# The output projection of a hybrid encoder layer: three PSUM banks in turn instead of two

## The chip, the cores and the metric

One core of a Trainium2 chip runs the whole layer as one program. The metric is the device time of one execution in microseconds (us), given as the median of several runs. A profile is one further execution, with a record of every instruction.

## What is computed

The layer normalises its input, projects it once into queries, keys, values and gates, runs windowed attention and a state-space scan beside each other, merges the two branches, and ends with an output projection, a residual sum and a second normalisation. Shapes: 2048 tokens, 1024 channels, float32.

```python
h = rms_norm(x, norm_gain[l])
proj = jnp.einsum('bsd,de->bse', h, w_in[l])
...
attn = windowed_gqa(q, k, v, attn_sink[l], rel_bias_table) * jax.nn.silu(z_attn)
y = s5_bidirectional(u_ssm, ...)
y = jax.nn.gelu(y)
y = y * jax.nn.sigmoid(jnp.einsum('bsc,ce->bse', y, w_glu[l]) + b_glu[l])
ssm = y * jax.nn.silu(z_ssm)
merged = jax.nn.sigmoid(g_attn) * jnp.einsum('bsc,cd->bsd', attn, w_branch_attn[l]) \
       + jax.nn.sigmoid(g_ssm) * jnp.einsum('bsc,cd->bsd', ssm, w_branch_ssm[l])
x = x + jnp.einsum('bsd,de->bse', merged, w_out[l])
return rms_norm(x, final_norm_gain)
```

## The kernel before

Every float32 matmul is made of three: each operand is split into a high and a low part of a narrower type, and high x high, high x low and low x high are summed in PSUM. The tokens are cut into four blocks of 512. The program goes through the input projections with normalisation, scan and attention worked in beside them, and then, for the blocks in the order 2, 3, 1, 0, through three stages:

- `glu(b)` (L1503): a 512 x 512 projection of the scan's output and the elementwise work around it, most of it on VectorE.
- `branch(b)` (L1530): both branch projections, gated and summed into `mh` and `ml` (the high and low part of `merged`).
- `outp(b)` (L1580): the output projection, which the change touches. For four tiles of 128 tokens (`t`) and two halves of the channels (`n`) it runs a group of 24 matmuls (L1592 to L1594, eight steps of three) into one PSUM bank. VectorE then adds the bank to the residual tile `xr` (L1599), and `finish` (L1627) squares, normalises and stores the tile on ScalarE, GpSimd and VectorE in later turns.

The loop at the end of the program runs `branch(b)`, then `glu` of the next block, then `outp(b)`, so that the weights and the gates of the next block are under way. Beside `branch` runs `gelu_prep` of the next block (L1415), and beside `outp(b)` runs `attn_prep` of the next block (L1466): it loads four tiles `ar` (L1474), copies each on ScalarE into a high part `ah` (L1484) and subtracts on VectorE for the low part `al` (L1485). The last `outp` (block 0) has no such companion.

The order of each engine's queue is the order of the program text; side work is dealt into it by `tick` and `turn`, which the matmul loops call at fixed points. An engine works off its queue in that order, so an addition L1599 stands behind whatever VectorE work was issued before it.

PSUM has eight banks, each of 128 x 512 float32. They are handed out by name, as the two lines below say: three called `pj`, two each called `s1` and `s2`, and one called `s3`. A new tile of a name takes the name's next bank, and its first matmul waits until the bank's last reader is done. In the profile all of `s1`, `s2` and `s3` appear as `s`. `s3` is used by attention's values alone (`values`, L1154; last read in `result`, L1179).

```python
PSB = {"pj": 3, "s1": 2, "s2": 2, "s3": 1}
...
return ps.tile([128, 512], F32, tag=tag, name=tag, bufs=PSB[tag])
```

Of the kernel before, what the change touches and what calls it, by code (L numbers as in the profile page):

```python
# [37 lines left out]
def kernel(  # L38
# [43 lines left out]
    def bank(tag):  # L82
        return ps.tile([128, 512], F32, tag=tag, name=tag, bufs=PSB[tag])
# [22 lines left out]
    def tick():  # L106

        flush()
        due = [f for n, f in laters if n <= 1]
        laters[:] = [(n - 1, f) for n, f in laters if n > 1]  # L110
        for f in due:
            f()
        turn()

    def turn():

        for sd in sides:
            if sd["done"]:
                continue
            sd["credit"] += 0.5 * sd["rate"]  # L120
            while sd["credit"] > 0.0:
                try:
                    sd["credit"] -= 0.5 if next(sd["gen"]) is HALF else 1.0
                except StopIteration:
                    sd["done"] = True
                    break
# [1119 lines left out]
    with tc.manual_schedule():  # L1246
# [55 lines left out]
        s2 = ExitStack()  # L1302
# [272 lines left out]
        def load_xr(b, t, q=None):  # L1575
            r0 = b * BLK + t * 128
            xrs[b, t] = ftile([128, D], F32, "xr", "xr", 3)
            (q or nc.sync).dma_start(out=xrs[b, t], in_=x[r0:r0 + 128, :])

        def outp(b, last):  # L1580
            mh, ml = mx.pop(b)
            for t in range(4):
                r0 = b * BLK + t * 128
                xr = xrs.pop((b, t))
                if t + 1 < 4:
                    load_xr(b, t + 1)
                for n in range(2):
                    pt = bank("s2")
                    cs = slice(n * 512, (n + 1) * 512)
                    for k in range(KD):  # L1590
                        ts_ = slice(t * 128, (t + 1) * 128)
                        PE.matmul(pt, mh[k][:, ts_], wo[0, n][:, k], start=k == 0, stop=False)  # L1592
                        PE.matmul(pt, mh[k][:, ts_], wo[1, n][:, k], start=False, stop=False)  # L1593
                        PE.matmul(pt, ml[k][:, ts_], wo[0, n][:, k], start=False, stop=k == KD - 1)  # L1594
                        if k == 3:
                            tick()
                        elif k % 4 == 1:
                            turn()
                    V.tensor_tensor(xr[:, cs], xr[:, cs], pt, ALU.add)  # L1599
                    if last and t == 3:  # L1600
                        finish_half(xr, r0, n)
                    tick()
                if not (last and t == 3):
                    finish(xr, r0)
# [3 lines left out]
        def finish_half(xr, r0, n):  # L1608

            cs = slice(n * BLK, (n + 1) * BLK)  # L1610
            if n == 0:
                sl_["sm"] = ftile([128, 3], F32, "sml", "sml")
                sl_["xf"] = ftile([128, D], F32, "xr", "xf", 3)
            sm, xf = sl_["sm"], sl_["xf"]
            A.activation(ttile("jk").bitcast(BF16)[:, 0:BLK], xr[:, cs], AF.Square, accum_out=sm[:, n:n + 1])
            V.tensor_tensor(xf[:, cs], xr[:, cs], fin["fg"][:, cs], ALU.mult)
            if n == 0:
                return
            V.tensor_tensor(sm[:, 2:3], sm[:, 0:1], sm[:, 1:2], ALU.add)
            V.tensor_scalar(sm[:, 2:3], sm[:, 2:3], 1.0 / D, 1e-6, ALU.mult, ALU.add)  # L1620
            Q.tensor_tensor(sm[:, 2:3], sm[:, 2:3], mhalf[:, 0:1], ALU.pow)
            V.tensor_scalar_mul(xf[:, 0:BLK], xf[:, 0:BLK], sm[:, 2:3])
            nc.sync.dma_start(out=out[r0:r0 + 128, 0:BLK], in_=xf[:, 0:BLK])
            A.activation(xf[:, BLK:D], xf[:, BLK:D], AF.Copy, scale=sm[:, 2:3])
            A.dma_start(out=out[r0:r0 + 128, BLK:D], in_=xf[:, BLK:D])

        def finish(xr, r0):  # L1627
            sm = ftile([128, 2], F32, "sm", "sm", 3)

            def f1():  # L1630
                jk = ttile("jk").bitcast(BF16)
                A.activation(jk, xr, AF.Square, accum_out=sm[:, 0:1])

            def f2():
                V.tensor_scalar(sm[:, 1:2], sm[:, 0:1], 1.0 / D, 1e-6, ALU.mult, ALU.add)  # L1635
                Q.tensor_tensor(sm[:, 1:2], sm[:, 1:2], mhalf[:, 0:1], ALU.pow)  # L1636

            def f3():
                V.scalar_tensor_tensor(xr, xr, sm[:, 1:2], fin["fg"], ALU.mult, ALU.mult)

            def f4():
                A.dma_start(out=out[r0:r0 + 128, :], in_=xr)

            f1()
            later(1, f2)
            later(2, f3)
            later(3, f4)
# [36 lines left out]
        for i, b in enumerate(BO):  # L1684
            nxt = BO[i + 1] if i + 1 < NBLK else None
            if nxt is not None:
                sg = add_side(gelu_prep(nxt, 1), 1.0)
            branch(b, nxt)
            if nxt is not None:
                drain(sg)  # L1690
            load_xr(b, 0, A)
            if nxt is not None:
                glu(nxt)
                sa = add_side(attn_prep(nxt, 1), 1.0)
            outp(b, nxt is None)
            if nxt is not None:
                drain(sa)
# [48 lines left out]
```

## Time and profile before

| | us |
|---|---|
| median of 3 runs | 1507.56 |
| lowest and highest run | 1506.02, 1509.10 |
| profiled execution | 1508.19 |
| span of the profiled execution, first to last instruction | 1506.4 |
| TensorE busy | 1418.1 |
| VectorE busy | 1041.8 |
| ScalarE busy | 659.9 |
| GpSimd busy | 637.9 |

The span of a profiled execution is a little shorter than its time, by what lies before the first and behind the last instruction. Busy times overlap, since the engines work beside each other. A group of instructions in the profile has its busy time, the mean of one in ns, and the idle time of its engine just before it, with the instruction that ended that idle time. Matmuls overlap: one takes 0.40 us by its record and the next starts 0.23 us behind it.

### The profile page before, as it was taken

The numbers are of one execution on the slowest core, as the hardware profiler recorded it, in microseconds if no ns is written. First come the engines' busy times: TensorE is split into PE (matmuls) and PEld (weight loads), VectorE is DVE, ScalarE is ACT, GpSimd is POOL, SyncE is SP. The second block draws the span as 40 slices with busy tenths as digits, with TensorE's granted clock in tenths as the row PEclk, the third lists the DMA queues.
The fourth block names the chain that finished last, engine by engine and source line by source line (L and its number), as shares of the span: only waits on it lengthen the run. The fifth ranks groups of instructions, "written<-read, shape, count | busy, mean of one in ns | idle before, by whom it ended". The sixth has DMA issues, their size and how long they took to land.

```text
span 1506.4 us, 19697 instructions
## 1 busy us (share of the span) xinstructions
PE 1418.1 (94%) x6933; PEld 1154.6 (77%) x6933; DVE 1041.8 (69%) x1954; ACT 659.9 (44%) x1213; POOL 637.9 (42%) x683
## 2 busy tenths in 40 slices
PE   7999779899999999899999999999988999999998
PEld 6787567777778777788888888888766877877886
DVE  2327977779788788647999998874577386385442
ACT  6332133433534444535666666754453243242111
POOL 5520187758678777622111111112376153252320
PEclk9999989989999999999999999999999999999999
DMA  8534222322332332554333333235776375375441
GB/s 264 157 98 95 64 81 72 100 91 76 113 105 88 109 105 88 152 175 127 92 91 92 101 96 91 90 102 148 211 212 193 98 196 181 114 182 166 117 122 70
DMA packets 240723, 185.47 MB, mean 123 GB/s; under 512 B 57921, under 2 KB 202433, under 8 KB 240625
## 3 DMA queue, kind: packets, MB, share of 16 engines
q10 hardware_dynamic: 118192, 107.89, 24.3%
q1 hardware_dynamic: 122432, 76.34, 17.1%
q8 instruction: 54, 0.88, 0.2%
q14 instruction: 45, 0.36, 0.1%
HBM read 126.56 MB, written 57.62 MB: 122 GB/s over the span
## 4 chain that ended last, share of the span: by engine, by line
PE 39%; DVE 26%; issue 7%; DMA 6%; ACT 5%; POOL 4%; ACTq 1%; DVEq 0%; POOLq 0%; SPq 0%
PE pj L220 7%; PE pj L222 7%; PE pj L221 7%; PE s L1592 3%; PE s L1593 3%; PE s L1594 3%; DVE Hl L891 2%; DMA yt<-yS 2%; DVE X L879 2%; PE s L1163 2%; DVE X L868 2%; PE s L1110 2%; DVE rt L867 2%; DVE X L870 2%; PE s L1147 2%
## 5 line engine op out<-in xcount | busy, mean ns | idle before, releaser
L155 POOL TENSOR_TENSOR wl<-raw,wh 128x256 fp32r<-128x256 f32 x380 | 355.0, 964 | 573.5 <-ACT wh L163 483.7
L220 PE MATMUL pj<-hh,wh 128*128 128x512 f32 x976 | 391.2, 401 | 0.0
L222 PE MATMUL pj<-hh,wl 128*128 128x512 f32 x976 | 385.7, 395 | 0.0
L221 PE MATMUL pj<-hl,wh 128*128 128x512 f32 x976 | 385.6, 395 | 0.0
L222 PEld LDWEIGHTS pj<-hh,wl 128*128 128x128 f32 x976 | 185.6, 190 | 41.0
L220 PEld LDWEIGHTS pj<-hh,wh 128*128 128x128 f32 x976 | 186.3, 191 | 34.0
L221 PEld LDWEIGHTS pj<-hl,wh 128*128 128x128 f32 x976 | 186.1, 191 | 34.3
L163 ACT ACTIVATE wh<-raw 128x1024 fp32r<-128x1024 f32 x96 | 100.7, 1051 | 23.4 <-DMA raw<-in_w_branch_ssm_dram 7.9
L1592 PE MATMUL s<-woh,mh 128*128 128x512 f32 x256 | 102.3, 400 | 6.7 <-DVE xr L1599 6.7
L1594 PE MATMUL s<-woh,ml 128*128 128x512 f32 x256 | 102.0, 398 | 0.0
L1593 PE MATMUL s<-wol,mh 128*128 128x512 f32 x256 | 101.9, 398 | 0.0
L1127 ACT ACTIVATE p<-p,sml 128x384 f32<-128x384 f32 (+1 forms) x128 | 75.8, 594 | 16.3 <-DVE sml L1123 16.1
L1636 POOL TENSOR_TENSOR sm<-sm,mhalf 128x1 f32<-128x1 f32 x15 | 8.3, 550 | 170.1 <-DVE sm L1635 133.4
L404 ACT ACTIVATE st<-pj,bg 128x512 f32<-128x512 f32 x64 | 43.8, 685 | 79.0 <-PE pj L222 69.3
L1111 DVE CUSTOM_DVE_ANT_0 p<-s,bias 128x384 f32<-128x384 f32 (+1 forms) x128 | 68.3, 535 | 13.7 <-PE s L1110 13.2
L1599 DVE TENSOR_TENSOR xr<-xr,s 128x512 f32<-128x512 f32 x32 | 21.9, 686 | 69.3 <-PE s L1594 69.3
L867 DVE TENSOR_TENSOR rt<-X,es 128x1020 f32<-128x1020 f32 x32 | 43.3, 1353 | 38.1 <-issue 14.4
L1152 DVE TENSOR_TENSOR pl<-s,ph 128x512 fp32r<-128x512 f32 x92 | 62.9, 683 | 4.2 <-ACT ph L1150 2.9
L1110 PE MATMUL s<-kst,qs 128*128 128x384 f32 (+1 forms) x256 | 65.7, 339 | 0.0
L1592 PEld LDWEIGHTS s<-woh,mh 128*128 128x128 f32 x256 | 48.5, 189 | 20.5 <-DVE xr L1599 8.9
L870 DVE TENSOR_TENSOR X<-X,rt 128x510 f32<-128x510 f32 x64 | 62.0, 1009 | 1.1
L891 DVE TENSOR_TENSOR Hl<-X,Hh 64x1024 fp32r<-64x1024 f32 x32 | 46.7, 1460 | 17.9 <-ACT Hh L886 17.4
(307 smaller groups left out, 3049.2 us busy)
## 6 DMA issues: line engine op xcount, KB each, us to landing
raw<-in_w_in_dram SPq DMA_DIRECT2D x59, 512.0 KB
gS<-st ACTq DMA_DIRECT2D x64, 256.0 KB
gt<-gS ACTq DMA_DIRECT2D x64, 256.0 KB
x<-in_x_dram SPq DMA_DIRECT2D x16, 512.0 KB
raw<-in_w_branch_attn_dram SPq DMA_DIRECT2D x32, 256.0 KB
raw<-in_w_branch_ssm_dram SPq DMA_DIRECT2D x32, 256.0 KB
out_dram<-xr ACTq DMA_DIRECT2D x15, 512.0 KB
xr<-in_x_dram SPq DMA_DIRECT2D x12, 512.0 KB
```

Of the source, the lines that this page charges most:

```text
L155: eng.tensor_tensor(lo[:, ks], r[:, ks], hi[:, ks].bitcast(F32), ALU.subtract)
L163: A.activation(res[0], r, AF.Copy)
L220: PE.matmul(pt, w[0][:, k], r[0][:, k], start=start and k == 0, stop=False)
L221: PE.matmul(pt, w[0][:, k], r[1][:, k], start=False, stop=False)
L222: PE.matmul(pt, w[1][:, k], r[0][:, k], start=False, stop=stop and k == kt - 1)
L870: V.tensor_tensor(X[:, :, r], X[:, :, r], t[:, :, r], ALU.add if r == back else ALU.subtract)
L891: V.tensor_tensor(H[1][rows], xv, H[0][rows].bitcast(F32), ALU.subtract)
L1110: PE.matmul(pt[:, 0:w], s["qs"][:, h], kst[:, r, kv, k0 * 128:k1 * 128], start=r == 0, stop=r == 1)
L1127: A.activation(p[:, h, 0:w], p[:, h, 0:w], AF.Exp, bias=nm[:, j:j + 1], accum_out=den[:, j:j + 1])
L1592: PE.matmul(pt, mh[k][:, ts_], wo[0, n][:, k], start=k == 0, stop=False)
L1593: PE.matmul(pt, mh[k][:, ts_], wo[1, n][:, k], start=False, stop=False)
L1594: PE.matmul(pt, ml[k][:, ts_], wo[0, n][:, k], start=False, stop=k == KD - 1)
```

## The change

The tile for a group of the output projection is no longer always a bank of the name `s2`. A group's number in its block is 2t + n; where that leaves 1 when divided by 3 the bank `s3` is taken.

```diff
@@ -1585,7 +1585,7 @@
                 if t + 1 < 4:
                     load_xr(b, t + 1)
                 for n in range(2):
-                    pt = bank("s2")
+                    pt = bank(("s2", "s3", "s2")[(2 * t + n) % 3])
                     cs = slice(n * 512, (n + 1) * 512)
                     for k in range(KD):
                         ts_ = slice(t * 128, (t + 1) * 128)
```

## Rows read from the trace of the kernel before

**Rows 1.** The page: TensorE's total, and the groups L1592 and L1599.

```profile
PE 1418.1 (94%) x6933; PEld 1154.6 (77%) x6933; DVE 1041.8 (69%) x1954; ACT 659.9 (44%) x1213; POOL 637.9 (42%) x683
...
L1592 PE MATMUL s<-woh,mh 128*128 128x512 f32 x256 | 102.3, 400 | 6.7 <-DVE xr L1599 6.7
...
L1599 DVE TENSOR_TENSOR xr<-xr,s 128x512 f32<-128x512 f32 x32 | 21.9, 686 | 69.3 <-PE s L1594 69.3
```

**Rows 2.** Stretches from:to: length, TensorE busy (instructions), granted clock, DMA; four `outp`.

```profile
1147.68:1196.25 48.57, 46.60 (x193) 0.96 0.37 123
1255.27:1302.26 46.99, 45.34 (x193) 1.00 0.37 123
1361.54:1409.93 48.39, 45.33 (x193) 1.00 0.36 120
1454.73:1499.52 44.79, 44.79 (x193) 1.00 0.17 59
```

**Rows 3.** Timeline of TensorE: start, duration, line, matmul, [idle before, releaser]; in `outp`.

```profile
1158.64 0.40 PE L1594 MATMUL s<-woh,ml 128*128 128x512 f32 x1
1161.01 0.50 PE L1592 MATMUL s<-woh,mh 128*128 128x512 f32 x1 [1.97 <-DVE xr L1599]
1161.35 0.40 PE L1593 MATMUL s<-wol,mh 128*128 128x512 f32 x1
...
1163.29 0.63 PE L1593 MATMUL s<-wol,mh 128*128 128x512 f32 x1
1163.72 0.63 PE L1594 MATMUL s<-woh,ml 128*128 128x512 f32 x1
...
1267.29 0.50 PE L1592 MATMUL s<-woh,mh 128*128 128x512 f32 x1 [0.67 <-DVE xr L1599]
...
1274.15 0.50 PE L1592 MATMUL s<-woh,mh 128*128 128x512 f32 x1 [0.99 <-DVE xr L1599]
...
1373.55 0.50 PE L1592 MATMUL s<-woh,mh 128*128 128x512 f32 x1 [0.65 <-DVE xr L1599]
...
1379.03 0.40 PE L1594 MATMUL s<-woh,ml 128*128 128x512 f32 x1
1381.84 0.50 PE L1592 MATMUL s<-woh,mh 128*128 128x512 f32 x1 [2.41 <-DVE xr L1599]
```

**Rows 4.** Stretches as in rows 2: behind the first stall, and around the longest.

```profile
1162.05:1165.42 3.37, 3.37 (x9) 0.50 1.02 406
...
1379.20:1382.60 3.40, 0.99 (x4) 1.00 0.02 6
```

**Rows 5.** Timeline of VectorE in `outp` of blocks 2, 3 and 1.

```profile
1160.27 0.68 DVE L1599 TENSOR_TENSOR xr<-xr,s 128x512 f32<-128x512 f32 x1
1166.35 0.69 DVE L1485 TENSOR_TENSOR al<-ar,ah 128x512 fp32r<-128x512 f32 x1 [5.39 <-ACT ah L1484]
1166.96 0.68 DVE L1599 TENSOR_TENSOR xr<-xr,s 128x512 f32<-128x512 f32 x1
...
1196.45 0.69 DVE L1599 TENSOR_TENSOR xr<-xr,s 128x512 f32<-128x512 f32 x1 [3.71 <-PE s L1594]
...
1273.41 0.68 DVE L1599 TENSOR_TENSOR xr<-xr,s 128x512 f32<-128x512 f32 x1
...
1381.10 0.68 DVE L1599 TENSOR_TENSOR xr<-xr,s 128x512 f32<-128x512 f32 x1
```

**Rows 6.** Timeline of ScalarE: the first `ah` in `outp` of block 1.

```profile
1379.83 0.63 ACT L1484 ACTIVATE ah<-ar 128x512 fp32r<-128x512 f32 x1 [7.65 <-DMA ar<-aS]
```

**Rows 7.** Timeline of TensorE: a stall outside `outp`, at the start of `glu`.

```profile
1246.30 0.50 PE L221 MATMUL pj<-gl,wh 128*128 128x512 f32 x1 [1.56 <-DVE gl L1446]
```

**Rows 8.** Line L1179: durations least/median/most, first and last start.

```profile
L1179 DVE TENSOR_TENSOR ob<-s,up x64: 408/417/421, 719.7 to 1017.3; 64x256 f32<-64x256 f32 x64
```

**Rows 9.** Stretches between the `outp`: length, VectorE busy (instructions), granted clock, DMA.

```profile
1196.25:1255.27 59.02, 44.12 (x53) 1.00 0.73 188
1302.26:1361.54 59.28, 44.18 (x53) 1.00 0.73 186
```

## The prediction

> **What bounds the kernel now.** I read the page first. TensorE is busy for 94% of the span [rows 1], so time is to be had only where it stands still or where its clock is low. The matmuls of the output projection (L1592) have 6.7 us of idle time in front of them, all put down to the addition L1599 that empties their PSUM bank; that addition in turn waits 69.3 us for TensorE over its 32 executions [rows 1]. Both at once means: on average VectorE is far ahead, and only in some places late.
>
> To see where, I cut out the four executions of `outp`, from the first matmul of each to the first one behind it, and read TensorE's busy time in each [rows 2]. They issue the same 192 matmuls each, and last 48.57, 46.99, 48.39 and 44.79 us. The last one (block 0) is without a gap: 44.79 us busy out of 44.79, so 44.79 / 192 = 0.2333 us from one matmul to the next, and 24 x 0.2333 = 5.60 us for a group (one bank). It has no `attn_prep` beside it. So the reader has the same work with and without the wait in one trace: the excess of the other three is 3.78 + 2.20 + 3.60 = 9.58 us.
>
> The timeline of TensorE shows what the excess is made of [rows 3]. In block 2 the last matmul of a group starts at 1158.64 and the next group's first at 1161.01: 2.37 us instead of 0.23, with another 0.11 us at the matmul behind it, so 2.25 us. This is more than the 1.97 us that the idle column gives, because the modelled end of a matmul (0.40 us behind its start) lies behind the point where the next could have begun. From 1162.05 to 1165.42 matmuls then start every 0.43 us [rows 3] at a granted clock of 0.50 [rows 4], the 1.2 GHz level: 8 intervals of about 0.19 us too much, 1.53 us. Together 3.78, the whole excess. Blocks 3 and 1 have two stalls each and no low clock: 0.94 + 1.26 us, and 0.92 + 2.68 us, counted in the same way. So there are five stalls, at the third group (1161.01, 1267.29, 1373.55) and twice at the fourth (1274.15, 1381.84).
>
> The timeline of VectorE says why the additions are late [rows 5]. The one of group 0 comes at 1160.27, behind the elementwise work that `glu` left queued; with two banks, group 2 needs that bank. The one of group 1 stands in VectorE's queue behind `al` (L1485), which waits for ScalarE's `ah`, and that for the load `ar` [rows 6]: VectorE idles 5.39 us before 1166.35, and the addition comes at 1166.96. Group 3 needs it. By the end of each `outp` VectorE waits for TensorE again, 3.71 us before the last addition [rows 5].
>
> **The change part by part.** Nothing is added or removed: the same matmuls, additions, loads and tiles, in the same order on every queue. Only the bank names change, and with them what the first matmul of a group waits for. The names of groups 0 to 7 are s2, s3, s2, s2, s3, s2, s2, s3. The two s2 banks alternate, five uses in a block, so every group waits for the addition three groups back instead of two.
>
> *Group 2 (third).* Its bank was last used in the block before, or is s3 itself, so the wait for group 0 goes: 2.25, 0.94 and 0.92 us. *Group 3* now needs group 0's addition. That starts at 1160.27 in block 2 and takes 0.69 us, while group 3 would begin at 1147.68 + 3 x 5.60 = 1164.48. It has 3.5 us to spare there, and the stalls of blocks 3 and 1 at this place, 1.26 and 2.68 us, go too. *Group 4* is what is late next: it needs group 1's addition, the one behind `al`. It would begin 22.40 us after the block's first matmul, at 1170.08, 1277.67 and 1383.94. The additions start at 1166.96, 1273.41 and 1381.10 [rows 5] and end 0.69 us later: 2.4, 3.6 and 2.2 us to spare. They are not moved by a faster TensorE, since what holds them is the load `ar` [rows 6]; nor does it start the load earlier, since that is issued by ScalarE in `glu`'s own sequence.
>
> *The low clock in block 2.* It follows the stall, the only idle time of TensorE since the block began, so without the stall I count the 1.53 us as gone. But an idle stretch does not always bring it: behind the longest stall (1379.03 to 1381.84) the clock stays at 1.00 [rows 4]. So which stalls pay this is not settled from run to run. The remaining stalls outside `outp`, such as the 1.56 us at 1246.30 [rows 7], come at other moments after the change, and one or two of them could pay 1.53 us each: 0 to +3.1 us. I take 0, since none of them does in these two blocks now.
>
> *The bank s3 itself.* Its last reader in attention (L1179) starts at 1017.3 [rows 8], 130 us before it is wanted, so its first use waits for nothing. A price for writing or emptying this bank rather than another is not shown for `outp`. The nearest row bounds it: block 0 changes its bank seven times without a gap [rows 2]. I take 0.
>
> *What follows `outp`.* The gain counts only if `branch` and `glu` start and end as much earlier. They are largely VectorE's work, 44.12 us busy out of 59.02 [rows 9], so VectorE could hold its end fixed. But VectorE itself starts `branch` waiting for TensorE [rows 5], so it starts earlier as well. The trace has a comparison: the two stretches between `outp`s last 59.02 and 59.28 us [rows 9], although the `outp` before the second was 1.58 us shorter than the one before the first [rows 2]. So a shorter `outp` gave back at most 0.26 of 1.58, a sixth. Of the 3.78 + 2.20 us that pass through such a stretch this is 0 to 1.0 us; I take 0. Behind the third, block 0 has a `branch` without preparation beside it, and the tail is unchanged.
>
> **Sum.** 2.25 + 1.53 + 2.20 + 3.60 = 9.58 us. The profiled execution took 1508.19 us (1506.4 us of span and 1.8 us around it), so 1498.6 us; it lies 0.6 us above the median of the runs, 1507.56, on which scale it is 1498.0. I give 1498.3.
>
> **The rivals.**
> *Given back in part.* The loads behind `branch` and `glu` (or `ar`, arriving later than the 2.2 us to spare) set the pace, and TensorE waits there instead. For it: VectorE is busy for three quarters of those stretches, and the addition of group 1 hangs on a load that took until 1379.83 with ScalarE waiting 7.65 us [rows 6]. Against it: the two equal stretches. With the one-sixth loss on all of it and two low-clock stretches of 1.53 us: 1498.3 + 1.6 + 3.1 = 1503.0; half of the gain lost gives the same.
>
> *It does not do what it says.* If the pool gave groups 2 and 3, and 5 and 6, the same s2 bank, each second one would wait for the addition just before it: 0.40 us to the end of the last matmul and 0.74 us from the addition to the next start (1160.27 to 1161.01), less 0.23, so 0.9 us, eight times: 7.3 us back, 1505.6, which is no change. Against it: in block 0 seven changes between the two s2 banks are without a gap, so the pool does alternate. Full cover elsewhere (all of the gain waited for later) gives 1507.5, no change as well.
>
> *Slower.* TensorE changes its bank with every group, and if each change cost enough to bring the clock down, `outp` would run partly at 1.2 GHz: 1.53 us for each low stretch as in block 2. It decides from (9.6 + 3.0) / 1.53, some eight such stretches among the 32 groups; one for every second group would be 1498.3 + 16 x 1.53 = 1522.8. Against it: block 0, seven changes, no gap, busy throughout [rows 2]. In the Trainium skill, "TensorE: Matmul & The Clock Gate", section "A second HAM failure mode: psum-queue depth-cycling", tells of such a kernel: cycling through PSUM banks idles TensorE a little between groups, and its clock swings between the two levels. By that rule this change, which cycles through more banks, would be the slower case; the trace does not agree, since the gaps here are those of a bank not yet empty, and more banks take them away.
>
> **How the numbers follow.** Forecast as summed, 1496 to 1501: 0.75. Given back in part, 1501 to 1505: 0.12. No change (either way): 0.06. Slower: 0.04. Faster still than 1496, when other runs than the profiled one pay the low clock more often: 0.03. A measurement of this kernel can tell about 0.2%, 3 us, from no change, so faster means below 1504.5: 0.75 + 0.03 + 0.10 = 0.88; same 0.08; slower 0.04. Range: below, the lowest run shown, 1506.02, less 9.6, is 1496.4, so 1496.0; above, it takes in the unknown costs up to half of their sum (1.0 and 3.1) and about half of the second case: 1502.5.
>
> **What would show it.** In the profile after: no wait of L1592 for L1599, or under 0.5 us in all; four `outp` stretches of 44.8 us each; no granted clock below 1.00 in them; the stretches between them still 59 us; the additions of groups 0 and 1 as late against the start of their block as now. Wrong would be a new wait before group 4 or 5, longer stretches between, or more low-clock matmuls in `branch` and `glu`.

## The result, and the profile after

The changed kernel takes 1498.02 us (median of 12 runs, 1496.32 to 1504.59), the kernel before in the same comparison 1506.76 us (12 runs, 1502.15 to 1510.3). The ratio is 0.995, with a 95% interval of 0.9937 to 0.9963: 8.7 us less by the medians, 7.5 us by the ratio, 5.6 to 9.5 us by its interval. The forecast was 1498.3 us.

The profiled execution took 1497.58 us, with a span of 1495.8 us. Both programs have the same instructions in the same order on every engine. So the two traces can be laid side by side stretch by stretch. Here are the four output projections of the changed kernel, which answer to [rows 2] (columns: from:to, length, TensorE busy and instructions, granted clock, DMA share and GB/s):

```profile
1146.29:1191.09 44.80, 44.80 (x194) 1.00 0.40 133
1250.53:1295.33 44.80, 44.80 (x194) 1.00 0.40 129
1354.49:1399.30 44.81, 44.81 (x194) 1.00 0.39 130
1444.09:1488.89 44.80, 44.80 (x193) 1.00 0.16 59
```

All four are alike now, busy throughout, at a granted clock of 1.00. Before they took 48.57, 46.99, 48.39 and 44.79 us. The difference, 3.77 + 2.19 + 3.58 = 9.54 us (0.01 more in the fourth), is the whole excess that the prediction had read off.

The page's groups, to be held against [rows 1]: idle time ahead of L1592 has gone from 6.7 us to nothing, and VectorE's wait for TensorE ahead of the addition from 69.3 to 60.0 us, by nearly what the groups were held up before.

```profile
L1592 PE MATMUL s<-woh,mh 128*128 128x512 f32 x256 | 101.3, 396 | 0.0
...
L1599 DVE TENSOR_TENSOR xr<-xr,s 128x512 f32<-128x512 f32 x32 | 21.9, 684 | 60.0 <-PE s L1594 60.0
```

TensorE's timeline in block 2 at the changes from group 1 to 2, 2 to 3 and 3 to 4 (start, duration, matmul; to be held against [rows 3]):

```profile
1157.25 0.40 PE L1594 MATMUL s<-woh,ml 128*128 128x512 f32 x1
1157.49 0.40 PE L1592 MATMUL s<-woh,mh 128*128 128x512 f32 x1
...
1162.85 0.40 PE L1594 MATMUL s<-woh,ml 128*128 128x512 f32 x1
1163.09 0.40 PE L1592 MATMUL s<-woh,mh 128*128 128x512 f32 x1
...
1168.45 0.40 PE L1594 MATMUL s<-woh,ml 128*128 128x512 f32 x1
1168.69 0.40 PE L1592 MATMUL s<-woh,mh 128*128 128x512 f32 x1
```

Each change takes 0.24 us, as any other matmul to the next. The additions are not any earlier. This is VectorE's timeline in block 1 (with the idle time before and its releaser in brackets), to be held against [rows 5]:

```profile
1365.76 0.68 DVE L1599 TENSOR_TENSOR xr<-xr,s 128x512 f32<-128x512 f32 x1
1373.32 0.69 DVE L1485 TENSOR_TENSOR al<-ar,ah 128x512 fp32r<-128x512 f32 x1 [6.88 <-ACT ah L1484]
1373.93 0.68 DVE L1599 TENSOR_TENSOR xr<-xr,s 128x512 f32<-128x512 f32 x1
```

The block begins at 1354.49, so the additions of groups 0 and 1 start 11.27 and 19.44 us into it. In the kernel before, the second one started 1381.10 - 1361.54 = 19.56 us in. VectorE is as late as it was, and behind the same wait; only nobody waits for it.

The stretches between the output projections, to be held against [rows 9] (VectorE busy):

```profile
1191.09:1250.53 59.44, 44.21 (x53) 1.00 0.74 186
1295.33:1354.49 59.16, 44.13 (x53) 1.00 0.71 187
```

59.44 and 59.16 us instead of 59.02 and 59.28: 0.42 us longer and 0.12 us shorter, so 0.3 us more in sum. That is no larger than what two profiles of one kernel differ by. In the second profile of the kernel before (described below) the same stretches are:

```profile
1194.59:1253.89 59.30, 44.11 (x53) 1.00 0.73 186
1300.95:1360.40 59.45, 44.19 (x53) 1.00 0.72 186
```

So it is not shown that anything was given back. The account between the two profiled spans, 1506.4 and 1495.8 us, is then: 9.53 us from the projections, 1.39 us because the first of them began earlier (1147.68 and 1146.29; nothing that runs before it was changed, and the second profile of the kernel before has 1146.29 too), less 0.3 us between the projections, and the rest (the last `branch` and the tail) unchanged.

### The profile page after: what moved, and what is told of

It is laid out like the page before. It is cut to its first block, busy times and chain, and to the rows that moved or that the text cites. A ratio compares the mean times of both kernels' runs of the same rounds, so it can differ in the third digit from the quotient of the medians.

```text
span 1495.8 us, 19697 instructions
## 1 busy us (share of the span) xinstructions
PE 1411.9 (94%) x6933; PEld 1151.1 (77%) x6933; DVE 1042.3 (70%) x1954; ACT 659.8 (44%) x1213; POOL 636.9 (43%) x683
## 4 chain that ended last, share of the span: by engine, by line
PE 45%; DVE 19%; POOL 7%; DMA 6%; issue 6%; ACT 4%; ACTq 1%; POOLq 0%; DVEq 0%; SPq 0%
PE pj L221 8%; PE pj L220 8%; PE pj L222 8%; PE s L1593 4%; PE s L1592 4%; PE s L1594 4%; POOL wl L155 3%; DMA yt<-yS 2%; PE s L1163 2%; DVE Hl L891 2%; PE s L1110 2%; PE s L1147 2%; DVE pl L1152 1%; PE s L858 1%; DVE X L879 1%
## 5 line engine op out<-in xcount | busy, mean ns | idle before, releaser
L1592 PE MATMUL s<-woh,mh 128*128 128x512 f32 x256 | 101.3, 396 | 0.0
L1599 DVE TENSOR_TENSOR xr<-xr,s 128x512 f32<-128x512 f32 x32 | 21.9, 684 | 60.0 <-PE s L1594 60.0
L1594 PEld LDWEIGHTS s<-woh,ml 128*128 128x128 f32 x256 | 48.1, 188 | 11.7
```

## The experiments

The kernels can be compared by one number that is steadier than the run's time: what passes from the first matmul of the first output projection to the end of the run (the profiled run's time less the start of that matmul; the 1.8 us outside the span are in all of them). For the changed kernel it is 1497.58 - 1146.29 = 351.3 us, for the kernel before 1508.19 - 1147.68 = 360.5 us. The experiments are edits of the kernel before, the last two of the changed kernel. Each ratio is to runs of the kernel before taken beside the experiment; their median is 1508.68 us, not 1506.76.

### Another bank as the third: is it something of s3?

```diff
-                    pt = bank("s2")
+                    pt = bank(("s2", "s1", "s2")[(2 * t + n) % 3])
```

> Here the third bank of the output projection is one of the two called s1 instead of s3; all else is the kernel before. My theory (only the number of banks between a group and its reuse counts, so that a group waits for the addition three groups back): as with s3, no wait before L1592 in the four stretches, each 44.8 us, time 0.6% below the kernel before, as the changed kernel's 1498 against 1507. Rival (something of s3 itself, its place in PSUM or that attention left it free long before, makes the gain): stalls remain or the time is over 1502.

Measured: 1501.98 us (6 runs, 1497.35 to 1503.72), ratio 0.9952 (0.9937 to 0.9968). Two of the four projections in its profile, in the columns as above (the others are 44.81 and 44.80):

```profile
1147.30:1192.10 44.80, 44.80 (x193) 1.00 0.41 133
1251.47:1296.28 44.81, 44.81 (x194) 1.00 0.40 129
```

The profiled run took 1498.53 us, 351.2 us from the first projection on, as the changed kernel. So the gain is not bound to s3; another third bank does as well. The median is higher than the expected 1498 us, but so is that of the kernel before beside it, and the ratio is that of the changed kernel.

### Four banks: does the wait only move?

```diff
-                    pt = bank("s2")
+                    pt = bank(("s2", "s1")[n])
```

> Four banks in turn (s2, s1, s2, s1), so each group waits for the addition four groups back. My theory (with three banks group 4 already has 2.2 to 3.6 us to spare, so nothing is left to take away): the same as the changed kernel, 44.8 us for each of the four stretches, 1498 within 2 us. Rival (the wait of the third bank is only moved, and a fourth takes away more): stretches shorter than those of the changed kernel by 1 us or more, time below 1495. Rival (each change of bank costs something): longer stretches than with three.

Measured: 1496.91 us (5 runs, 1496.23 to 1497.39), ratio 0.9924 (0.9912 to 0.9937). The projections:

```profile
1145.08:1189.89 44.81, 44.81 (x194) 1.00 0.41 134
1249.32:1294.13 44.81, 44.81 (x194) 1.00 0.39 129
1353.16:1397.96 44.80, 44.80 (x193) 1.00 0.39 130
1442.76:1487.56 44.80, 44.80 (x193) 1.00 0.17 59
```

The stretches are those of three banks to 0.01 us: nothing more is gained, and one more bank has no price. The profiled run took 1496.23 us, 351.15 us from the first projection on, as the changed kernel. By the runs this kernel is the fastest (ratio 0.9924 against 0.995 for the changed kernel, with intervals that just touch). The profile shows no such difference from the first projection on, and before it the two programs are the same; where it comes from, if it is one, is not shown.

### The third bank once in a block: where is it needed?

```diff
-                    pt = bank("s2")
+                    pt = bank("s3" if (t, n) == (1, 0) else "s2")
```

> The bank s3 is used for group 2 alone, once in a block; the other seven groups alternate between the two s2 banks. So groups 2, 3 and 4 wait three groups back, and groups 5 to 7 two groups back as before. My theory (the stalls lie at groups 2 and 3 alone): as the changed kernel, four stretches of 44.8 us, 1498 within 2 us. Rival (the third bank is also needed later, because TensorE now runs further ahead of VectorE): a new wait at group 5 or 6, in block 1 above all, where the addition of group 3 ends at about 1388.5 and group 5 would begin at 1389.5 by the times of the kernel before; up to 1 us for each block.

Measured: 1500.15 us (6 runs, 1494.44 to 1503.04), ratio 0.9943 (0.9925 to 0.9961). The projections:

```profile
1149.54:1194.33 44.79, 44.79 (x193) 1.00 0.40 134
1253.51:1298.31 44.80, 44.80 (x193) 1.00 0.39 129
1357.13:1401.93 44.80, 44.80 (x194) 1.00 0.40 130
1446.72:1491.52 44.80, 44.80 (x193) 1.00 0.17 59
```

One use of the third bank in each block, at group 2, does all of it, and no wait appears at groups 5 to 7, which go back to two banks. The rival, that TensorE would now run into VectorE later in the block, falls. The profiled run took 1500.19 us, 350.65 us from the first projection on.

### Two banks, but the second addition ahead of `al`: one cause or two?

```diff
-                sa = add_side(attn_prep(nxt, 1), 1.0)
+                sa = add_side(attn_prep(nxt, 2), 1.0)
```

> Two banks as before, but the preparation beside the output projection starts one step later, so that the addition of group 1 stands in VectorE's queue ahead of the first al instead of behind it. My theory of the two causes (group 2 stalls on elementwise work of the stage before, group 3 on al and its load): the stalls at group 3, 1.26 us in block 3 and 2.68 us in block 1, go; those at group 2 (2.25, 0.94, 0.92 us) stay. Stretches of about 48.6 (47.1 if the low clock is not met), 45.7 and 45.7 us instead of 48.6, 47.0 and 48.4; time 3.9 us below the kernel before. Rival (all five stalls have one cause, VectorE being behind as a whole): the stall at group 3 stays, or moves to group 4, and the time is that of the kernel before within 1.5 us.

Measured: 1502.53 us (7 runs, 1499.5 to 1504.98), ratio 0.9961 (0.9947 to 0.9975). The projections, and VectorE's timeline in block 1 ("x2": two additions merged into one row):

```profile
1145.97:1194.56 48.59, 46.61 (x194) 0.96 0.38 123
1253.93:1299.62 45.69, 45.07 (x193) 1.00 0.40 127
1358.67:1404.39 45.72, 45.07 (x194) 1.00 0.40 127
1449.19:1493.98 44.79, 44.79 (x193) 1.00 0.16 59
```

```profile
1369.95 1.28 DVE L1599 TENSOR_TENSOR xr<-xr,s 128x512 f32<-128x512 f32 x2
1377.68 0.69 DVE L1485 TENSOR_TENSOR al<-ar,ah 128x512 fp32r<-128x512 f32 x1 [6.45 <-ACT ah L1484]
```

The second addition follows the first at once, and the wait of 6.45 us for `ah` stands behind both. The stretches of blocks 3 and 1 fall to 45.69 and 45.72 us, as expected to 0.02 us: the stalls at group 3 are gone, those at group 2 (0.9 us each) stay. The medians fell by 6.2 us where 3.9 was expected (3.8 to 8.0 by the interval); from the first projection to the end of the profiled run it is 1502.66 - 1145.97 = 356.7 us, 3.8 less than in the kernel before. Two causes, then, and one spare bank covers both. That the cause at group 2 is the work left by `glu` is read from VectorE's queue [rows 5]; no run moved that work.

### One bank: what does a late bank cost, and what does the clock make of it?

```diff
-                    pt = bank("s2")
+                    pt = bank("s3")
```

> All groups of the output projection in the one bank s3, so each group waits for the addition just before it: the opposite of the change, to measure what a late bank costs and to test the rival that the clock suffers at each change of bank. By the rows of the kernel before a change of bank then costs about 1.06 us where VectorE is idle (0.43 us from the last matmul to the addition, 0.69 us for it, 0.06 us to the next matmul, 0.11 us at the one behind, less 0.23), 28 times, and in blocks 2, 3 and 1 group 1 waits for the addition of group 0, 7.7, 6.4 and 6.4 us, less the 1.06 counted. Stretches of about 59, 58, 59 and 52.2 us, time 1547 to 1556 with a low-clock stretch or two after the long waits. Rival (idle time at every change of bank brings the clock down): low granted clock in most groups, some 1.5 us for each, stretches of 60 us in block 0 and over 65 in the others, time over 1580.

Measured: 1553.82 us (2 runs, 1551.85 and 1555.78), ratio 1.0307 (1.028 to 1.0333). The projections, and three rows of TensorE's timeline (block 2 at groups 1 and 2, block 0 at group 1):

```profile
1150.31:1211.56 61.25, 49.03 (x194) 0.92 0.30 98
1270.81:1330.88 60.07, 49.16 (x193) 0.94 0.28 97
1389.94:1450.17 60.23, 49.31 (x193) 0.94 0.29 97
1494.97:1547.11 52.14, 46.68 (x193) 1.00 0.14 51
```

```profile
1163.62 0.80 PE L1592 MATMUL s<-woh,mh 128*128 128x512 f32 x1 [7.54 <-DVE xr L1599]
1172.63 0.49 PE L1592 MATMUL s<-woh,mh 128*128 128x512 f32 x1 [0.78 <-DVE xr L1599]
...
1501.52 0.49 PE L1592 MATMUL s<-woh,mh 128*128 128x512 f32 x1 [0.78 <-DVE xr L1599]
```

Block 0: (52.14 - 44.79) / 7 = 1.05 us for a change of bank that waits for its addition, where 1.06 was worked out from the rows before; 52.2 us was expected for the stretch, and the time is within the 1547 to 1556 us expected. The granted clock there stays at 1.00 through seven such idle times. In the other three blocks it falls, to means of 0.92 and 0.94, and by the timeline only behind the first wait (6.23 to 7.54 us of idle time), not at the later changes. Their stretches are 1.2 to 2.3 us longer than the 59, 58 and 59 us expected. So the rival in which the clock suffers at each change of bank, and with it the slower case of the prediction, has no support here, even with an idle time at each change. The section of the Trainium skill that the prediction weighed ("TensorE: Matmul & The Clock Gate", "A second HAM failure mode: psum-queue depth-cycling") describes clock swings from small idle times between groups of matmuls. Block 0 of this run shows none, with 0.78 us of idle time in every 6.65 us.

### The kernel before, once more

No edit.

> The kernel before once more, for a second profile of it. My theory (the five stalls come from the order of the queues, so they recur to within 0.1 us; the low clock depends on more than the stall): stretches of 47.0 or 48.6, 47.0, 48.4 and 44.8 us. If the low clock in block 2 belongs to that stall, 48.6 comes again; if it comes at random behind such stalls, it is as likely to be missing there or to stand in block 1.

Measured: 1508.41 us in the one run. The projections, two rows of TensorE's timeline in block 2, and one behind the long stall of block 1:

```profile
1146.29:1194.59 48.30, 45.34 (x193) 1.00 0.38 125
1253.89:1300.95 47.06, 45.33 (x194) 1.00 0.37 124
1360.40:1410.14 49.74, 46.72 (x193) 0.97 0.36 117
1454.94:1499.74 44.80, 44.80 (x193) 1.00 0.17 59
```

```profile
1159.62 0.50 PE L1592 MATMUL s<-woh,mh 128*128 128x512 f32 x1 [1.96 <-DVE xr L1599]
1166.49 0.50 PE L1592 MATMUL s<-woh,mh 128*128 128x512 f32 x1 [1.00 <-DVE xr L1599]
...
1380.65 0.79 PE L1592 MATMUL s<-woh,mh 128*128 128x512 f32 x1 [2.37 <-DVE xr L1599]
```

The stalls recur: 1.96 us of idle time where [rows 3] has 1.97, and 2.37 where it has 2.41. The low clock does not: in block 2 the clock stays at 1.00 this time, and it falls in block 1 (mean 0.97), behind the stall of 2.37 us, where it stayed up in the first profile. It is not bound to one of the stalls. And there is a sixth stall, at group 3 of block 2 (1166.49, 1.00 us of idle time), that the first profile does not have. The low clock had hidden it: with TensorE at 1.2 GHz for some matmuls, group 2 ended later than the addition that group 3 needs. In the first profile that addition starts at 1166.96 and takes 0.68 us [rows 5], and group 3 begins behind it, without a wait:

```profile
1168.25 0.40 PE L1592 MATMUL s<-woh,mh 128*128 128x512 f32 x1
```

With the low clock the stretch took 48.57 us, without it 48.30, where I had expected 47.0. So the 1.53 us of low clock cost 0.27 us there, not 1.53. In block 1, where no later wait was there to take it up, the stretch with the low clock is 1.35 us longer (49.74 and 48.39). The excess of this second profile over 44.80 is 3.50 + 2.26 + 4.94 = 10.7 us, of the first 9.6: what the change gives depends on where the low clock falls.

### Can the next wait be taken too?

The largest wait of TensorE that is left in this part of the changed kernel is for `gl` at the start of `glu` (1.54 and 1.57 us between the projections, 2.10 us ahead of the first; as in [rows 7]). Two kernels deal out `gelu_prep` faster beside `branch`, on top of the change, at 1.2 and 1.4 times the rate.

```diff
-                sg = add_side(gelu_prep(nxt, 1), 1.0)
+                sg = add_side(gelu_prep(nxt, 1), 1.2)
```

> The changed kernel (three banks), with the preparation of the next block's glu dealt out 1.2 times as fast beside the branch stage. It aims at the largest wait that TensorE has left after the change, 1.5 to 2.1 us for gl at the start of each glu. My theory (gl is late only because its steps end with the last group of branch): the wait goes at the two glu stages inside the block loop, 59.3 us between two output projections becomes 57.5, and the time falls by 3 to 4 us to about 1494.5. Rival (VectorE has no room, so what is done earlier for glu delays the additions of branch): the wait turns into one for the gates' banks, the stretches stay at 59.3 or grow, the time is 1498 or more.

> As the kernel with rate 1.2, with 1.4. My theory: as with 1.2, nothing more to gain, 57.5 us between two output projections and about 1494.5; if the loads yt need the slots of the tiles that output still reads, ScalarE's queue stands and it is 1 to 3 us worse than 1.2. Rival (VectorE has no room): longer stretches than with 1.2.

Measured: 1518.22 us (6 runs, 1515.6 to 1520.08) with 1.2, ratio to the kernel before 1.007 (1.0054 to 1.0086); 1509.23 us (12 runs, 1503.97 to 1513.98) with 1.4, ratio 1.0006 (0.9989 to 1.0023). By the ratios (0.995 for the changed kernel) both are slower than the changed kernel, by some 18 and 8 us, and my theory falls. With 1.2 the stretches between the projections are 65 us instead of 59, 10.9 us in all (first fence: columns TensorE, its weight loads, VectorE, ScalarE, GpSimd, clock, DMA). Another 7.3 us lie ahead of the first projection, where `branch` has `gelu_prep` beside it too: from the first matmul of `sh` there to the projection it is 67.7 us (1090.23 to 1157.94) instead of 60.5 (1085.84 to 1146.29). ScalarE's timeline in the first stretch between projections, and then TensorE's, show why:

```profile
1202.74:1267.70 64.96, 58.27 (x241) 45.69 (x240) 45.16 (x53) 25.88 (x34) 32.47 (x34) 0.97 0.63 165
1312.51:1377.02 64.51, 58.27 (x241) 45.67 (x240) 44.57 (x52) 25.42 (x34) 31.71 (x34) 0.97 0.63 163
```

```profile
1226.62 1.06 ACTq L1423 DMA_DIRECT2D yt<-yS  x1
1228.68 0.63 ACT L1442 ACTIVATE gh<-yt 128x512 fp32r<-128x512 f32 x1 [2.28 <-DMA gt<-gS]
1233.53 1.06 ACT L1429 ACTIVATE yt<-yt 128x512 f32<-128x512 f32 x1 [4.22 <-DMA yt<-yS]
...
1234.50 1.04 ACT L163 ACTIVATE wh<-raw 128x1024 fp32r<-128x1024 f32 x1
```

```profile
1235.59 0.80 PE L220 MATMUL pj<-ah,wh 128*128 128x512 f32 x1 [4.69 <-ACT wh L163]
```

The wait for `gl` is gone, and in its place TensorE waits for the split of its next weights: the square of a tile `yt`, dealt out too early, holds ScalarE for 4.22 us until its load has landed, and the split `wh` stands behind it in ScalarE's queue. The granted clock falls to a mean of 0.97 in both stretches besides. With 1.2, neither of the two mechanisms I had named (a gain, or VectorE without room) is what happened. For 1.4 I had also named a standing ScalarE queue, behind loads `yt` that wait for their tiles, and a time no better than with 1.2; it is 9 us better. There the waits for `wh` from 1100 us on sum to 8.9 us instead of 18.5, and the stretches between the projections are 59.49 and 61.13 us. Most of its loss lies ahead of the first projection, 67.3 us from the first matmul of `sh` (1087.67 to 1154.98), and its trace has the same pair of waits there (ScalarE's row, then TensorE's):

```profile
1095.89 1.06 ACT L1429 ACTIVATE yt<-yt 128x512 f32<-128x512 f32 x1 [8.28 <-DMA yt<-yS]
...
1097.96 0.80 PE L220 MATMUL pj<-ah,wh 128*128 128x512 f32 x1 [6.04 <-ACT wh L163]
```

No run issued the loads `yt` earlier, so it is not shown that this alone would win the wait for `gl`.

## Why the prediction was right

**What bounds it.** The four stretches with equal work, one of them without a gap, gave in the first profile the sum of what could be won before any mechanism was named: 9.58 us, of which the profile after has 9.53. That part did not rest on the idle column, which had 6.7 us.

**The waits that go.** They went at groups 2 and 3, as the prediction had it, and the run with the late `attn_prep` separated the two causes.

**What is late next.** Group 4 was to have 2.4, 3.6 and 2.2 us to spare. In the profile after, the addition of group 1 in block 1 starts 19.44 us into the block and takes 0.69; group 4 begins at 22.40: 2.3 us. No projection has a gap any more, and four banks make none of them shorter.

**The low clock.** The sum was right and the step partly wrong. I counted 1.53 us as its price and the wait of group 3 in block 2 as absent. The second profile of the kernel before shows that the two take each other's place: without the low clock, 1.17 + 0.11 us of stall come instead. The term for block 2 is 2.25 us for the first stall and then either 1.53 or 1.28, so it comes to about the same by luck.

**Given back.** 0 to 1.0 us was the bound, 0 taken. The 0.3 us between the two profiles is within what two profiles of the kernel before differ by, so 0 has held as far as these traces can tell. The bound had been read from two stretches of one trace, whose difference of 0.26 us is no larger than that either.

**The slower rival and the bank s3.** The one-bank kernel gave the price of a change of bank that waits for its addition, 1.05 us, and in block 0 no fall of the clock with it; s1 does as well as s3.

**The size of the gain.** 9.6 us was forecast on the profile's scale, and the medians show 8.7, the ratio 7.5 (5.6 to 9.5), so the forecast gain lies at the upper end, just outside. That the time agrees with the forecast to 0.3 us is partly luck: the median of the kernel before, 1507.56 in three runs, was 1506.76 in the twelve of the comparison.

## What to carry to other kernels

Where a stage runs several times with the same work and one of the executions has nothing beside it and no gap, its length is the floor of the others, and the difference is the most that removing waits can give; start-to-start times show it in full, the idle column does not. A queue that is late only for a moment can be covered by one more buffer at that moment, without a deeper rotation throughout: here one use of a third bank per block gave all of it, and a fourth bank nothing. Before side work is moved earlier, look at what stands behind it in its queue: a step that must wait for its load holds everything there.

## What the runs showed of the hardware that I had not expected

The low clock after a stall of about 2 us comes in one execution and not in the next. Three profiles with two banks (the kernel before twice, and the late preparation) met it in block 2, in block 1 and in block 2. It cost 0.27 us where a slower TensorE was about to wait anyway, and 1.35 us where it was not. What decides it was not tested.

The spread of run times, 8 us among the twelve runs of the changed kernel, does not show in the part that was changed. In the profiles of four kernels whose projections are alike to 0.02 us, the first projection begins between 1145.08 and 1149.54 us, and from there to the end of the run it is 350.65 to 351.3 us in each; the programs up to that point are the same. So a few us between medians of five or six runs, such as 1501.98 and 1496.91 us for the two versions with s1, can't be put down to the projections. What makes the earlier part longer or shorter was not looked into.
